# Sliding-window attention on one core: the value products of a unit directly ahead of the next unit's transposes

## The chip, the core and the metric

One core of one Trainium2 chip runs the whole program. The metric is the device time of one execution in microseconds (us); a kernel's time is the median of several runs. One execution was also recorded by the hardware profiler; times of single instructions come from there.

The engines are named as in the profile: PE (TensorE, matmuls; PEld is its weight load), DVE (VectorE), ACT (ScalarE), POOL (GpSimd) and SP (SyncE, which starts the loads). Each has an instruction queue of its own; between them semaphores keep the order of data.

## What is computed

The reference is a trunk of two layers on x of 1024 tokens by 1024 channels, in float32. The first is a gated MLP, cut here; the second is windowed attention with sinks:

```python
q, z = jnp.split(h @ w_in, 2, axis=-1)
...
logits = jnp.einsum('btkgd,bskd->bkgts', qb, kb).astype(jnp.float32) + alibi
valid = in_window & ((start - BLOCK + c) >= 0)
logits = jnp.where(valid, logits, -jnp.inf)
m = jnp.maximum(jnp.max(logits, axis=-1), sink)
p = jnp.exp(logits - m[..., None])
denom = jnp.sum(p, axis=-1) + jnp.exp(sink - m)
o = jnp.einsum('bkgts,bskd->btkgd', p.astype(vb.dtype), vb).astype(jnp.float32)
o = o / denom.transpose(0, 3, 1, 2)[..., None]
...
y = out * jax.nn.silu(z)
return y @ w_out
```

There are 16 query heads of 64 channels over 4 key/value heads, blocks of 128 queries, and a window of 128 keys, so a query sees its own block up to itself and the rest of its window in the block before.

## The kernel before

Large products are made with each operand split in a high and a low part, three matmuls in place of one (`mm3`, L169 to L171). The gated MLP takes the first three quarters of the time. In the attention stage, keys kh and kl, values vt and queries q are held in on-chip memory.

The attention of a half of the tokens (`attn`, L1114) is cut in eight units, one for each of two pairs of key/value heads (p) and four blocks of queries (b). Names carry b_p: s5_1 are the scores of block 5, pair 1. A unit has four steps.

- **Scores** (L1037 to L1075), in two halves gp of eight matmuls (L1058), over two banks of PSUM each (s5_1_00 and s5_1_01, then s5_1_10 and s5_1_11). DVE merges the window's two key blocks (copy_predicated, L1063) and takes bias and minimum (L1069), ACT the exponential (L1073).
- **Normalise** (L1078, L1079), on DVE.
- **Transposes** (L1081 to L1091): eight on PE (L1086) into two banks pt; ACT copies each bank into pc (L1087). POOL then masks pp, the earlier key block, out of pc (L1090), and pc itself (L1091). Units of blocks 0 have no pp.
- **Values** (L1093 to L1113): for each of two halves par of the array's columns a matmul with pc (L1105) and one with pp (L1107) into bank o; DVE multiplies by z (L1111), and the result is split for the output projection, q_hi on ACT (L105) and q_lo on DVE (L106).

The tiles s, o and pt draw their banks from one pool of four ("s"); the products that fill up have four others ("mm"). pc and pp share a tag with two buffers.

The steps of three units are interleaved. In turn i of the loop (L1125 to L1136) stand the first score half of unit i, the values of unit i-2, two calls of `more()`, the transposes of unit i-1, and the second score half and normalise of unit i. Each call of `more()` draws steps from a generator of other work: the projections of the next q and z, the shared keys and values, and at the end the output projection. These are the filling products: qz, pk and pv, ob, 128x512 or 128x256 matmuls. A unit's turn has mostly eighteen of them at each of the places where they are drawn.

The program written in this order goes through a scheduler, which may place instructions of an engine otherwise, by its own estimate of when operands are ready, and which sets the bank of each tile and the waits. What stands on each engine is shown below where it differs.

Of the kernel before, what the change touches and what calls it, by code (L numbers as in the profile page):

```python
# [34 lines left out]
def step(*gens):  # L35
    for g in gens:
        next(g, None)
# [13 lines left out]
def tile_yoco(  # L51
# [1062 lines left out]
    def attn(h, q, z, fill, total, late=0):  # L1114
        taken = [0, 0]
        n = 34 if late else 40

        def more():
            taken[0] += 1
            while taken[1] < min(total, total * taken[0] / n) + late * max(0, taken[0] - n):  # L1120
                taken[1] += 1
                step(fill)

        units = [Unit(b, p, q, z) for p in range(2) for b in range(4 * h, 4 * h + 4)]
        for i in range(len(units) + 2):  # L1125
            if i < len(units):
                units[i].scores(0)
            if 0 <= i - 2:
                units[i - 2].values()
            more()  # L1130
            more()
            if 0 <= i - 1 < len(units):
                units[i - 1].transposes()
            if i < len(units):
                units[i].scores(1)
                units[i].normalise()  # L1136
            more()
            more()
# [89 lines left out]
    q1 = pair("P3", "q1")  # L1228
    fill = chain(kv_phase(1, n1), q_phase(1, n1, q1), z_phase(1, n1, z1, 0, 4))
    attn(0, q0, z0, fill, 64)  # L1230
    drain(fill)

# [4 lines left out]

    fill = chain(z_phase(1, n1, z1, 4, 8), tail())
    attn(1, q1, z1, fill, 48, 2)
    drain(fill)  # L1240

# [60 lines left out]
```

## Time and profile before

| what | value |
| --- | --- |
| median of 3 runs | 1050.24 us (1049.72 to 1050.43) |
| the profiled execution, its own time | 1051.19 us |
| its span in the profile | 1049.4 us |
| granted clock of the core | 0.998 |
| first score matmul / last value block begins | 769.03 / 1002.36 us of the span |

The profiled execution is 0.95 us longer than the median of the runs, and 1.8 us of it lie around the span. An engine's busy time includes overlap between matmuls that follow each other, so how fast PE goes is read from the starts of two rows, and not from their lengths. In rows of the timeline the first number is the start in us from the span's beginning, the second the busy time in us; "x4" groups instructions of one kind.

### The profile page before, as it was taken

The numbers are of one execution on the slowest core, as the hardware profiler recorded it, in microseconds if no ns is written. First come the engines' busy times: TensorE is split into PE (matmuls) and PEld (weight loads), VectorE is DVE, ScalarE is ACT, GpSimd is POOL, SyncE is SP. The second block draws the span as 40 slices with busy tenths as digits, with TensorE's granted clock in tenths as the row PEclk, the third lists the DMA queues.
The fourth block names the chain that finished last, engine by engine and source line by source line (L and its number), as shares of the span: only waits on it lengthen the run. The fifth ranks groups of instructions, "written<-read, shape, count | busy, mean of one in ns | idle before, by whom it ended". The sixth has DMA issues, their size and how long they took to land.

```text
span 1049.4 us, 13678 instructions
## 1 busy us (share of the span) xinstructions
PE 1038.2 (99%) x4994; PEld 854.8 (81%) x4994; DVE 731.8 (70%) x1244; ACT 579.8 (55%) x998; POOL 199.5 (19%) x153
## 2 busy tenths in 40 slices
PE   9999999999999999999999999999999999999997
PEld 7878888888888888888888888888888777877776
DVE  6987566867768668677696587765247786667763
ACT  6584344565565465655444465654466665786631
POOL 0500003253442552530200000100001111011120
PEclk9999999999999999999999999999999999999999
DMA  8878242324333333247998543532322121211363
GB/s 309 271 262 292 101 171 94 116 101 146 126 117 120 123 134 116 101 140 265 320 354 282 195 167 93 200 102 82 99 81 66 56 81 61 81 61 62 121 220 121
DMA packets 80899, 157.56 MB, mean 150 GB/s; under 512 B 5824, under 2 KB 32704, under 8 KB 80832
## 3 DMA queue, kind: packets, MB, share of 16 engines
q1 hardware_dynamic: 76320, 148.01, 41.4%
q10 hardware_dynamic: 4512, 8.68, 2.3%
q8 instruction: 39, 0.64, 0.3%
q14 instruction: 28, 0.23, 0.1%
HBM read 125.21 MB, written 31.46 MB: 149 GB/s over the span
## 4 chain that ended last, share of the span: by engine, by line
PE 93%; DVE 3%; DMA 2%; ACT 1%; issue 0%; SPq 0%; DVEq 0%; POOLq 0%; ACTq 0%
PE qz L169 6%; PE ob L169 6%; PE ub L169 6%; PE qz L171 6%; PE ub L170 6%; PE ub L171 6%; PE ob L171 6%; PE ob L170 6%; PE qz L170 6%; PE s L1058 3%; PE uc L170 3%; PE uc L169 3%; PE uc L171 3%; PE sp L621 3%; PE oc L169 2%; PE oc L171 2%
## 5 line engine op out<-in xcount | busy, mean ns | idle before, releaser
L110 DVE SCALAR_TENSOR_TENSOR wlo<-raw_w,gn,whi 128x512 fp32r<-128x512 f32 x80 | 58.5, 757 | 62.2 <-ACT whi L109 62.0
L169 PE MATMUL qz<-n_hi,whi 128*128 128x512 f32 x256 | 100.9, 394 | 0.0
L171 PE MATMUL qz<-n_hi,wlo 128*128 128x512 f32 x256 | 99.8, 390 | 1.1 <-DVE wlo L110 1.1
L170 PE MATMUL qz<-n_lo,whi 128*128 128x512 f32 x256 | 99.9, 390 | 0.0
L109 ACT ACTIVATE whi<-raw_w,gn 128x512 fp32r<-128x512 f32 x80 | 54.8, 716 | 56.8 <-PE qz L170 36.6
L1073 ACT ACTIVATE pr<-pr,mx 128x129 f32<-128x129 f32 x128 | 50.1, 393 | 39.8 <-DVE mx L1069 39.8
L169 PEld LDWEIGHTS qz<-n_hi,whi 128*128 128x128 f32 x256 | 48.1, 188 | 15.8 <-issue 5.7
L105 ACT ACTIVATE uzhilo_g<-f 128x1024 fp32r<-128x1024 f32 x31 | 32.9, 1060 | 49.2 <-PE uc L171 43.3
L171 PEld LDWEIGHTS qz<-n_hi,wlo 128*128 128x128 f32 x256 | 48.0, 188 | 11.8 <-DVE wlo L110 1.5
L170 PEld LDWEIGHTS qz<-n_lo,whi 128*128 128x128 f32 x256 | 48.1, 188 | 9.3
L106 DVE TENSOR_TENSOR uzhilo_g<-f,uzhilo_g 128x1024 fp32r<-128x1024 f32 x31 | 38.6, 1245 | 19.9 <-ACT uzhilo_g L105 19.9
L209 ACT ACTIVATE uz_slots<-ub 128x512 f32<-128x512 f32 x48 | 28.3, 590 | 42.4 <-PE ub L171 39.2
L169 PE MATMUL ub<-T,whi_g 128*128 128x512 f32 x128 | 50.7, 396 | 0.0
L169 PE MATMUL ub<-T,uzhilo_g 128*128 128x512 f32 x128 | 50.5, 395 | 0.0
L171 PE MATMUL ub<-T,wlo_g 128*128 128x512 f32 x128 | 49.9, 390 | 0.0
L171 PE MATMUL ub<-T,uzhilo_g 128*128 128x512 f32 x128 | 49.9, 390 | 0.0
L170 PE MATMUL ub<-T,uzhilo_g 128*128 128x512 f32 x128 | 49.9, 390 | 0.0
L170 PE MATMUL ub<-T,whi_g 128*128 128x512 f32 x128 | 49.8, 389 | 0.0
L169 PE MATMUL uc<-T,uzhilo_g 128*128 128x512 f32 x124 | 48.9, 395 | 0.0
L170 PE MATMUL uc<-T,uzhilo_g 128*128 128x512 f32 x124 | 48.3, 389 | 0.0
L171 PE MATMUL uc<-T,uzhilo_g 128*128 128x512 f32 x124 | 48.3, 389 | 0.0
L105 ACT ACTIVATE whi_g<-raw_uz 128x1024 fp32r<-128x1024 f32 (+1 forms) x31 | 26.5, 854 | 36.8 <-PE ua L170 14.3
(334 smaller groups left out, 3078.3 us busy)
## 6 DMA issues: line engine op xcount, KB each, us to landing
raw_uz<-in_wuz_in_dram SPq DMA_DIRECT2D x32, 512.0 KB, 3.4
raw_w<-in_wqz_dram SPq DMA_DIRECT2D x32, 512.0 KB, 3.5
td<-uz_slots SPq DMA_DIRECT2D x56, 256.0 KB, 2.2
orawP2a<-td SPq DMA_DIRECT2D x28, 512.0 KB, 4.1
raw<-in_wv_in_dram SPq DMA_DIRECT2D x17, 512.0 KB, 4.8
vg<-vd SPq DMA_DIRECT2D x8, 1024.0 KB, 5.3
orawP2b<-in_wo_a_dram SPq DMA_DIRECT2D x16, 512.0 KB, 8.2
vraw<-in_wv_in_dram SPq DMA_DIRECT2D x13, 512.0 KB, 4.8
```

Source lines behind the costliest of these rows:

```text
L105: nc.scalar.activation(hi, src, AF.Copy)
L106: nc.vector.tensor_tensor(lo, src, hi.bitcast(F32), ALU.subtract)
L109: nc.scalar.activation(hi, src, AF.Copy, scale=g)
L110: nc.vector.scalar_tensor_tensor(lo, src, g, hi.bitcast(F32), ALU.mult, ALU.subtract)
L169: nc.tensor.matmul(out, lhsT=a_hi, rhs=b_hi, start=start, stop=False, skip_group_check=True)
L170: nc.tensor.matmul(out, lhsT=a_hi, rhs=b_lo, start=False, stop=False, skip_group_check=True)
L171: nc.tensor.matmul(out, lhsT=a_lo, rhs=b_hi, start=False, stop=stop, skip_group_check=True)
L209: nc.scalar.activation(out, a, AF.Copy)
L621: nc.tensor.matmul(psv[:, n], lhsT=d["vg"][:, 4 * j + n, i * P:(i + 1) * P], rhs=d["wc"], start=True, stop=True)
L1058: nc.tensor.matmul(pss[par][:, g, w0:256], lhsT=q[par][:, m, bs_], rhs=w[par][:, p, ks], start=g + k == 0, stop=g + k == 2, skip_group_che ...
L1073: nc.scalar.activation(pr[:, i], pr[:, i], AF.Exp, bias=mx[:, i:i + 1], scale=-1.0, accum_out=dn[:, i:i + 1])
```

## The change

The two calls of `more()` move ahead of the values of unit i-2. The first score half of unit i is now followed by filling products, then by the values of unit i-2 and directly by the transposes of unit i-1 and the second score half of unit i.

```diff
@@ -1125,10 +1125,10 @@
         for i in range(len(units) + 2):
             if i < len(units):
                 units[i].scores(0)
+            more()
+            more()
             if 0 <= i - 2:
                 units[i - 2].values()
-            more()
-            more()
             if 0 <= i - 1 < len(units):
                 units[i - 1].transposes()
             if i < len(units):
```

The first place is PE in the second pair of the first half: o1_1 are the values of unit 1_1, pt2_1 the transposes of 2_1, s3_1 the scores of 3_1, qz1 filling products (the number at the end of a name is a buffer's). Before, the values stand behind the first scores and ahead of the filling products:

```order
L1058 MATMUL s3_1_01_6766<-kh1_4959,q0_lo_4970 128x256
L1058 MATMUL s3_1_01_6766<-kl1_5556,q0_lo_4970 128x256
L1105 MATMUL o1_1_6785<-pc1_1_6693,vt_4968 64x512
L1107 MATMUL o1_1_6785<-pp1_1_6706,vt_4968 64x512
L1105 MATMUL o1_1_6785<-pc1_1_6693,vt_4968 64x512
L1107 MATMUL o1_1_6785<-pp1_1_6706,vt_4968 64x512
L169 MATMUL qz1_0_5_6540<-n1_hi_5306,whi31_6673 128x512
L170 MATMUL qz1_0_5_6540<-n1_lo_5307,whi31_6673 128x512
```

and, eighteen filling matmuls further, the transposes follow on these, with the second scores behind them:

```order
L170 MATMUL qz1_0_7_6542<-n1_lo_5307,whi31_6673 128x512
L171 MATMUL qz1_0_7_6542<-n1_hi_5306,wlo31_6674 128x512
L1086 MATMUL pt2_1_0_6824<-ident_82,pr2_1_6637 128x128 x4
L1086 MATMUL pt2_1_1_6830<-ident_82,pr2_1_6637 128x128 x4
L1058 MATMUL s3_1_10_6839<-kh0_4958,q0_hi_4969 128x256
L1058 MATMUL s3_1_10_6839<-kl0_4960,q0_hi_4969 128x256
L1058 MATMUL s3_1_11_6840<-kh1_4959,q0_lo_4970 128x256
L1058 MATMUL s3_1_11_6840<-kl1_5556,q0_lo_4970 128x256
L1058 MATMUL s3_1_10_6839<-kh0_4958,q0_hi_4969 128x256
L1058 MATMUL s3_1_10_6839<-kl0_4960,q0_hi_4969 128x256
```

In the changed kernel the same place reads:

```order
L170 MATMUL qz1_0_7_6534<-n1_lo_5307,whi31_6667 128x512
L171 MATMUL qz1_0_7_6534<-n1_hi_5306,wlo31_6668 128x512
L1105 MATMUL o1_1_6815<-pc1_1_6693,vt_4968 64x512
L1107 MATMUL o1_1_6815<-pp1_1_6706,vt_4968 64x512
L1105 MATMUL o1_1_6815<-pc1_1_6693,vt_4968 64x512
L1107 MATMUL o1_1_6815<-pp1_1_6706,vt_4968 64x512
L1086 MATMUL pt2_1_0_6824<-ident_82,pr2_1_6637 128x128 x4
L1086 MATMUL pt2_1_1_6830<-ident_82,pr2_1_6637 128x128 x4
L1058 MATMUL s3_1_10_6839<-kh0_4958,q0_hi_4969 128x256
L1058 MATMUL s3_1_10_6839<-kl0_4960,q0_hi_4969 128x256
L1058 MATMUL s3_1_10_6839<-kh0_4958,q0_hi_4969 128x256
L1058 MATMUL s3_1_10_6839<-kl0_4960,q0_hi_4969 128x256
```

The values stand between the last filling product and the transposes. The tiles of the second scores are also filled in another order: s3_1_10 wholly ahead of s3_1_11, where before they took turns.

The second place is PE further on, in the second half: o4_1 are the values of unit 4_1, ob0 filling products of the output projection. Before, twelve filling matmuls stand ahead of the first scores of 6_1, and the four value products stand together:

```order
L1058 MATMUL s6_1_01_7720<-kl1_5556,q1_lo_5850 128x256
L1058 MATMUL s6_1_00_7719<-kh0_4958,q1_hi_5849 128x256
L1058 MATMUL s6_1_00_7719<-kl0_4960,q1_hi_5849 128x256
L1058 MATMUL s6_1_01_7720<-kh1_4959,q1_lo_5850 128x256
L1058 MATMUL s6_1_01_7720<-kl1_5556,q1_lo_5850 128x256
L1105 MATMUL o4_1_7739<-pc4_1_7642,vt_4968 64x512
L1107 MATMUL o4_1_7739<-pp4_1_7655,vt_4968 64x512
L1105 MATMUL o4_1_7739<-pc4_1_7642,vt_4968 64x512
L1107 MATMUL o4_1_7739<-pp4_1_7655,vt_4968 64x512
L169 MATMUL ob0_1_0_7693<-whi44_7580,q0_hi_4969 128x512
L170 MATMUL ob0_1_0_7693<-wlo44_7581,q0_hi_4969 128x512
```

In the changed kernel the first scores of 6_1 follow at once on the second ones of 5_1, and of the values one product stands there alone:

```order
L1058 MATMUL s5_1_11_7659<-kl1_5556,q1_lo_5850 128x256
L1058 MATMUL s6_1_00_7719<-kh0_4958,q1_hi_5849 128x256
L1058 MATMUL s6_1_00_7719<-kl0_4960,q1_hi_5849 128x256
L1058 MATMUL s6_1_01_7720<-kh1_4959,q1_lo_5850 128x256
L1058 MATMUL s6_1_01_7720<-kl1_5556,q1_lo_5850 128x256
L1058 MATMUL s6_1_00_7719<-kh0_4958,q1_hi_5849 128x256
L1058 MATMUL s6_1_00_7719<-kl0_4960,q1_hi_5849 128x256
L1058 MATMUL s6_1_01_7720<-kh1_4959,q1_lo_5850 128x256
L1058 MATMUL s6_1_01_7720<-kl1_5556,q1_lo_5850 128x256
L1105 MATMUL o4_1_7761<-pc4_1_7642,vt_4968 64x512
L169 MATMUL ob0_1_0_7693<-whi44_7580,q0_hi_4969 128x512
L170 MATMUL ob0_1_0_7693<-wlo44_7581,q0_hi_4969 128x512
```

The other three come thirty filling matmuls later, ahead of the next unit's transposes:

```order
L170 MATMUL ob0_1_1_7694<-wlo45_7698,q0_hi_4969 128x512
L171 MATMUL ob0_1_1_7694<-whi45_7697,q0_lo_4970 128x512
L1107 MATMUL o4_1_7761<-pp4_1_7655,vt_4968 64x512
L1105 MATMUL o4_1_7761<-pc4_1_7642,vt_4968 64x512
L1107 MATMUL o4_1_7761<-pp4_1_7655,vt_4968 64x512
L1086 MATMUL pt5_1_0_7770<-ident_82,pr5_1_7592 128x128 x4
L1086 MATMUL pt5_1_1_7776<-ident_82,pr5_1_7592 128x128 x4
```

So the values of 4_1 are in two pieces in the changed kernel, and the filling matmuls that parted the two score blocks have moved behind the first piece.

The third place is DVE at the values of unit 2_0 (o2_0; wlo28 is a weight half of the filling products, L980 an evacuation of filling products). Before:

```order
L1069 ISA mx0_1_6378 128x1
L1111 TENSOR_TENSOR z0_0_5308<-o2_0_6401,z0_0_5308 128x4x128
L106 TENSOR_TENSOR q0_lo_4970<-z0_0_5308,q0_hi_4969 128x4x128
L110 SCALAR_TENSOR_TENSOR wlo28_6422<-raw_w28_6293,gn_80,whi28_6421 128x4x128 x2
L1046 COPY pr1_1_6507<-snk_4965 128x8
L980 SCALAR_TENSOR_TENSOR q1_hi_5849<-qz1_0_0_6219,qsc_4963,q1_hi_5849 64x512
L980 SCALAR_TENSOR_TENSOR q1_lo_5850<-qz1_0_0_6219,qsc_4963,q1_lo_5850 64x512
L1063 COPY_PREDICATED s0_1_10_6455<-mrg_4956,neg_4961 128x2x128
```

In the changed kernel:

```order
L1069 ISA mx0_1_6378 128x1
L110 SCALAR_TENSOR_TENSOR wlo28_6414<-raw_w28_6285,gn_80,whi28_6413 128x4x128 x2
L980 SCALAR_TENSOR_TENSOR q1_hi_5849<-qz1_0_0_6219,qsc_4963,q1_hi_5849 64x512
L980 SCALAR_TENSOR_TENSOR q1_lo_5850<-qz1_0_0_6219,qsc_4963,q1_lo_5850 64x512
L1111 TENSOR_TENSOR z0_0_5308<-o2_0_6431,z0_0_5308 128x4x128
L1046 COPY pr1_1_6507<-snk_4965 128x8
L106 TENSOR_TENSOR q0_lo_4970<-z0_0_5308,q0_hi_4969 128x4x128
L1063 COPY_PREDICATED s0_1_10_6455<-mrg_4956,neg_4961 128x2x128
L1063 COPY_PREDICATED s0_1_11_6456<-mrg_4956,neg_4961 128x2x128
```

The multiply L1111 has moved behind the weight split and the first evacuation, and stands nearer to the second scores of 0_1.

## Prediction, made before the changed kernel was run

> **What bounds the kernel now.** I read the page first: the busy shares, then the chain of work that ended last.
>
> ```profile
> PE 1038.2 (99%) x4994; PEld 854.8 (81%) x4994; DVE 731.8 (70%) x1244; ACT 579.8 (55%) x998; POOL 199.5 (19%) x153
> PE 93%; DVE 3%; DMA 2%; ACT 1%; issue 0%; SPq 0%; DVEq 0%; POOLq 0%; ACTq 0%
> ```
>
> TensorE is busy all the span and carries the chain. The next view is the table of stretches over the attention stage (span, PE, PEld, DVE, ACT, POOL, then the granted clock).
>
> ```profile
> core 0: us, PE busy (x) PEld busy (x) DVE busy (x) ACT busy (x) POOL busy (x), PEclk, DMA share, GB/s
> 800.00:820.00 20.00, 20.00 (x105) 15.77 (x105) 15.54 (x48) 13.10 (x39) 4.38 (x4) 1.00 0.17 54
> 900.00:920.00 20.00, 20.00 (x106) 15.97 (x105) 15.22 (x52) 12.68 (x44) 2.19 (x2) 1.00 0.24 79
> 980.00:1000.00 20.00, 20.00 (x100) 14.89 (x97) 14.26 (x34) 11.84 (x34) 4.69 (x5) 1.00 0.34 108
> ```
>
> PE fills 20.00 of 20.00 at clock 1.00 where the units run; no row of PE there names a wait. So nothing that the change could take out of a wait exists: the stage is the sum of its matmuls plus what is lost when PE passes from one kind of product to another. The change can gain only at such passages, and can lose wherever a product is now asked for before its operand or bank is ready. DVE is at about three quarters and ACT at two thirds, in order, so neither answers at once.
>
> The passages are read from start to start in the timeline of PE.
>
> ```profile
> 883.46 0.39 PE L170 MATMUL qz<-n_lo,whi 128*128 128x512 f32 x1
> 883.69 0.39 PE L171 MATMUL qz<-n_hi,wlo 128*128 128x512 f32 x1
> 884.01 1.08 PE L1105 MATMUL o<-pc,vt 128*64 128x512 f32 x4
> 884.92 1.03 PE L1107 MATMUL o<-pp,vt 128*64 128x512 f32 x4
> 885.88 0.50 PE L169 MATMUL qz<-n_hi,whi 128*128 128x512 f32 x1
> 886.22 0.40 PE L170 MATMUL qz<-n_lo,whi 128*128 128x512 f32 x1
> 886.46 0.40 PE L171 MATMUL qz<-n_hi,wlo 128*128 128x512 f32 x1
> ```
>
> A filling product starts 0.23 us after the one before. Into the value products it takes 0.32 (883.69 to 884.01), 0.09 too much; the block lasts 1.87 (to 885.88); and the first filling product behind it takes 0.34, 0.11 too much.
>
> **The change part by part.** The work is the same: as many instructions on each engine, in another order. SP's queue keeps its order.
>
> Regular passages. Before, a unit went scores, values, filling, transposes, scores; now scores, filling, values, transposes, scores. The entry of 0.09 stays (this row is itself one from filling into values). The 0.11 behind the values now falls on the first transpose. The difference is 0, with -0.11 x 15 = -1.6 as the good end (the load for the transposes hides) and, by the same size, +1.6 as the bad one. I take 0, since a transpose needs its 128x128 load just as the filling product did.
> The Trainium skill, "TensorEngine Tiling (Array Packing)", section "Key Properties", says that changing the tiling mode drains TensorE. By it the number of changes counts, and that number is the same before and after except at one unit (below), so the sum would be the same 0.
>
> The split unit. In the new order the values of unit 4_1 come apart: one product (pc, first column half), thirty filling matmuls, then the other three. The halves normally run side by side; a unit of block 0, which has only the pc pair, shows what one pass by itself lasts.
>
> ```profile
> 792.96 1.08 PE L1105 MATMUL o<-pc,vt 128*64 128x512 f32 x4
> 793.97 0.38 PE L169 MATMUL pv<-whi,n_hi 128*128 128x256 f32 x1
> ```
>
> The lone product costs 793.97 - 792.96 = 1.01, and the extra entry and exit 0.09 + 0.11: **+1.2 us**. Its remaining three still need two passes, so nothing comes back. Low end 0.2, if the three pair up better than I see.
>
> The same product comes too early. The twelve filling matmuls between scores(1) of 5_1 and scores(0) of 6_1 have gone behind it, so PE arrives soon after the transposes of 4_1, while POOL still masks. The rows of unit 5_1 give the offsets with ACT free: PE (first transposes, then the first, third, fifth of the eight score matmuls, then filling), ACT with the group of its line, POOL.
>
> ```profile
> 972.07 1.04 PE L1086 MATMUL pt<-ident,pr 128*128 128x128 f32 x8
> 972.86 0.36 PE L1058 MATMUL s<-kh,q_hi 128*128 128x256 f32 x1
> 973.18 0.28 PE L1058 MATMUL s<-kh,q_lo 128*128 128x256 f32 x1
> 973.41 0.28 PE L1058 MATMUL s<-kh,q_hi 128*128 128x256 f32 x1
> 973.89 0.40 PE L169 MATMUL ob<-whi,q_hi 128*128 128x512 f32 x1
> ```
> ```profile
> 972.78 1.09 ACT L1087 ACTIVATE pc<-pt 128x512 f32<-128x512 f32 x2 [0.61 <-PE pt L1086]
> L1087 ACT ACTIVATE pc<-pt x32: 573/595/601, 786.5 to 997.9; 128x512 f32<-128x512 f32 x32
> ```
> ```profile
> 973.94 1.10 POOL L1090 TENSOR_SCALAR_AFFINE_SELECT pp<-pc 128x1024 f32<-128x1024 f32 x1 [9.26 <-ACT pc L1087]
> 975.11 1.09 POOL L1091 TENSOR_SCALAR_AFFINE_SELECT pc<-pc 128x1024 f32<-128x1024 f32 x1
> ```
>
> POOL does pp first and ends pc at 976.20, 4.13 after the transposes began. PE reaches the lone product after 0.79 (transposes) + 1.03 + 1.03 (two score blocks) + 0.09 = 2.94. **+1.2 us** of stall; low end 0 if scores(0) of 6_1 are themselves late and take up the time, high end 2.2 if ACT's copies come a whole select later.
>
> The scores behind the transposes. The pool of banks for these tiles has four, and in the new built order five score blocks (units 0_1, 1_1, 3_1, 5_1, 6_1) take, for their second tile, the bank of the first transpose tile just before, instead of a bank long free. It is free when ACT's first copy ends: 972.78 + 0.595 = 973.38, 1.31 after the transposes began. The second tile is wanted by the third matmul (973.18, +1.11) in 0_1, 1_1 and 6_1 and by the fifth (973.41, +1.34) in 3_1 and 5_1. With 0.16 for the signal and the weight load behind the wait (an estimate, half of the 0.32 that the first two score matmuls take, 972.86 to 973.18), a third place costs 1.31 + 0.16 - 1.11 = 0.36 and a fifth 0.13, if ACT is free. It was not at three of them (the first transposes' row on PE, then ACT's rows, for the transposes ahead of 0_1, 1_1 and 3_1):
>
> ```profile
> 825.72 1.04 PE L1086 MATMUL pt<-ident,pr 128*128 128x128 f32 x8
> 826.62 0.68 ACT L976 ACTIVATE q_lo<-qz,qsc 64x512 fp32r<-64x512 f32 x1
> 827.33 1.09 ACT L1087 ACTIVATE pc<-pt 128x512 f32<-128x512 f32 x2
> 840.13 1.04 PE L1086 MATMUL pt<-ident,pr 128*128 128x128 f32 x8
> 840.60 0.62 ACT L105 ACTIVATE q_hi<-z 128x512 fp32r<-128x512 f32 x1
> 841.12 1.32 ACT L109 ACTIVATE whi<-raw_w,gn 128x512 fp32r<-128x512 f32 x2
> 842.46 1.09 ACT L1087 ACTIVATE pc<-pt 128x512 f32<-128x512 f32 x2
> 865.43 1.04 PE L1086 MATMUL pt<-ident,pr 128*128 128x128 f32 x8
> 867.88 0.69 ACT L976 ACTIVATE q_lo<-qz,qsc 64x512 fp32r<-64x512 f32 x1
> 868.59 1.09 ACT L1087 ACTIVATE pc<-pt 128x512 f32<-128x512 f32 x2
> ```
>
> At 825.72 the copy waited behind evacuations of the last filling products; these now finish 1.87 ahead of the transposes, so ACT is free: 0.36. At 840.13 the split q_hi goes behind the copy, but whi stays ahead: 842.46 - 0.52 = 841.94, plus 0.60 and 0.16, against 840.13 + 0.36 (the stall before it) + 1.11 = 841.60: 1.1. At 865.43 one of two evacuation pairs still stands ahead; the copy moves up from 868.59 by 0.5 and a pair of 1.4, to about 866.7 plus 0.76, against 866.77: about 0.7. Sum 0.36 + 1.1 + 0.7 + 0.13 + 0.36 = **+2.65 us**. The low end, ACT free everywhere, is 3 x 0.36 + 2 x 0.13 = 1.3; the high end, copies as late behind the transposes as before, has 827.33, 842.46 and 868.59, each plus 0.76, less 826.83, 841.24 and 866.77 at those places: 1.3 + 2.0 + 2.6, with 0.13 + 0.36 for the others 6.3.
>
> The multiply of the values. In most other units the second score tile takes the bank of the value product just finished, so it waits for DVE's multiply.
>
> ```profile
> 886.01 0.69 DVE L1111 TENSOR_TENSOR z<-o,z 128x512 f32<-128x512 f32 x1 [1.73 <-PE o L1107]
> 839.74 0.68 DVE L1111 TENSOR_TENSOR z<-o,z 128x512 f32<-128x512 f32 x1
> 832.67 1.09 PE L1105 MATMUL o<-pc,vt 128*64 128x512 f32 x4
> ```
>
> In these rows stand two multiplies of DVE and, for the second, the start of its value block on PE. With DVE free the multiply ends at 886.70, 2.69 after the block began at 884.01; the third score matmul comes at 1.87 + 1.11 = 2.98. It just fits; in the new order the multiply stands behind work that is done by then. I take **+0.2 us**, from 0 up to a single place like 839.74: 840.42 - 832.67 - 2.98 = 4.8.
>
> What follows on DVE and ACT (q_lo and q_hi of the values' output) comes a filling block later, and its reader is the output projection of a whole half later: nothing. At the end of the program the last filling products are as many.
>
> Sum: 1.2 + 1.2 + 2.65 + 0.2 = **+5.25 us**. The profiled execution took 1051.19 (span 1049.4), 0.95 above the median, so its own forecast is 1056.4; for the median 1050.24 + 5.25 = **1055.5**.
>
> **The rivals.** A measurement here tells about 0.2%, 2.1 us, from no change: below 1048.1 is faster, above 1052.3 slower.
>
> First, no difference: the waits are covered, since the score matmuls ahead of the copy start late enough or the copies come earlier, and only the split's 1.2 stays: 1051.4. For it: PE had no wait at all before, with scores behind the transposes there too. Against it: before, their banks had been released by values eighteen matmuls back. Chance 0.17.
>
> Second, faster: values and transposes are both 4-byte products on the same side of the filling, and the exit (0.11) and entry (0.09) vanish at fifteen units: -3.0. It decides only if the waits too are covered: 1047.2. For it: transposes behind filling showed no exposed load, so their load is hidden there. Against it: the o tiles are 128*64 and pt's 128*128. Chance 0.08.
> The Trainium skill, "TensorE: Matmul & The Clock Gate", section on the array's architecture, has the weight load pulled ahead of running matmuls; by that the 0.11 would vanish, -1.6. The 0.34 behind the values speaks against it here, since that load was not pulled ahead.
>
> Third, a bigger loss: DVE comes late to one multiply, as at 839.74, and PE stands 4.8, less the 0.2 already counted: 1060.1. It decides from the point at which DVE is more than 0.3 behind. Chance 0.13, and 0.62 for the forecast with its own range of 1052.5 to 1058.
>
> **How the numbers follow.** The likeliest case gives 1055.5. The range takes the no-change case's 1051.4 in and stops at 1050.8 (the split with the good end of the passages, 1050.24 + 1.2 - 1.6 = 1049.8, is half left out); upward it reaches 1059.2, where ACT's high end (6.3 instead of 2.65) ends: 1055.5 + 3.65 = 1059.2. Left out: the faster case and most of the late multiply. Faster 0.07, same 0.2 (the no-change case and some of the forecast's low end), slower 0.73.
>
> **What would show it.** In the new profile PE rows should name ACT's L1087 as what the scores waited for, at five units, some 0.1 to 1 us each, and POOL's L1091 ahead of the lone product of 4_1, about 1.2; the block of 4_1 should appear as 1.0 and 1.9. The start of the first transpose behind the values should be 1.87 after the block began, and the block itself 0.79 plus at most 0.11. The forecast is wrong if PE stays at 20.00 in every stretch with no wait (then the first rival, or the second if the whole stage is shorter), and short if waits on L1111 turn up.

## The result, and the profile after the change

The changed kernel takes 1057.49 us (median of 4 runs, 1057.26 to 1057.79) against 1050.34 (4 runs beside it): a ratio of 1.0066, 95% interval 1.0054 to 1.0078, so 7.15 us slower. The profiled execution took 1057.36 with a span of 1055.3, 5.9 above the 1049.4 of before; the rest of the 7.15 is that before's profiled run was slower than its median (0.85), that the changed kernel's was faster than its own (0.13), and 0.27 around the span. The last matmul starts at 1048.14 instead of 1042.26, and the first score matmul within 0.1 us of where it did, so the 5.9 us all arise in the attention stage.

In the page's first and fourth part PE still holds the span, but the chain of work that ended last has less of it.

```profile
PE 1041.5 (99%) x4994; PEld 854.1 (81%) x4994; DVE 735.7 (70%) x1244; ACT 579.7 (55%) x998; POOL 199.0 (19%) x153
PE 86%; DVE 6%; DMA 3%; ACT 2%; issue 1%; POOL 0%; SPq 0%; DVEq 0%; POOLq 0%; ACTq 0%
```

PE's share of the chain fell from 93% to 86%, and DVE's rose from 3% to 6%: there are now stretches in which the end is set by something PE waits for. The view of PE's waits, empty for this stage before, names three kinds (us in total, times, longest):

```profile
PE o L1105 <- POOL pc L1091: 1.5, 1, 1.5
PE qz L169 <- DVE q_lo L980: 0.8, 1, 0.8
PE s L1058 <- ACT pc L1087: 0.6, 2, 0.5
```

The view of the weight loads (PEld) shows the same waits and more, since a load can stand still without a matmul's row naming it:

```profile
PEld s L1058 <- ACT pc L1087: 1.8, 5, 0.7
PEld qz L169 <- DVE kl L1027: 0.8, 2, 0.5
```

Five score blocks wait for ACT's first copy, as predicted (their loads stand at 827.47, 843.55, 869.69, 964.64 and 979.11, in units 0_1, 1_1, 3_1, 5_1 and 6_1). The table of stretches shows where time is lost:

```profile
820.00:840.00 20.00, 19.06 (x93) 13.97 (x92) 17.02 (x44) 13.29 (x33) 2.62 (x2) 1.00 0.16 53
860.00:880.00 20.00, 19.53 (x98) 14.92 (x98) 17.78 (x41) 14.01 (x33) 2.18 (x2) 1.00 0.19 60
900.00:920.00 20.00, 20.00 (x109) 17.26 (x108) 13.14 (x44) 13.17 (x42) 2.18 (x2) 1.00 0.25 79
960.00:980.00 20.00, 18.41 (x93) 12.28 (x92) 13.85 (x37) 12.41 (x38) 2.90 (x3) 1.00 0.26 93
```

PE is 0.94 short of the full time in the first of these stretches, 0.47 in the second, 1.59 in the last, and full in others, as in the third. The busy time hides part of the loss, since a matmul's row is longer than its step: starts have to be compared. The timeline of PE at unit 4_1, and POOL's beside it:

```profile
966.06 0.28 PE L1058 MATMUL s<-kl,q_lo 128*128 128x256 f32 x1
967.79 1.07 PE L1105 MATMUL o<-pc,vt 128*64 128x512 f32 x2 [1.45 <-POOL pc L1091]
968.79 0.50 PE L169 MATMUL ob<-whi,q_hi 128*128 128x512 f32 x1
969.13 0.39 PE L170 MATMUL ob<-wlo,q_hi 128*128 128x512 f32 x1
```
```profile
965.15 1.09 POOL L1090 TENSOR_SCALAR_AFFINE_SELECT pp<-pc 128x1024 f32<-128x1024 f32 x1 [10.40 <-ACT pc L1087]
966.31 1.43 POOL L1091 TENSOR_SCALAR_AFFINE_SELECT pc<-pc 128x1024 f32<-128x1024 f32 x1
```

The lone product starts 1.73 after the last score matmul, where 0.21 is the usual step, and the moment is the end of POOL's mask (967.74): 1.5 us. Its block then lasts 1.00 by itself.

At the scores behind transposes, the longest wait is at unit 3_1, PE and ACT:

```profile
867.64 1.09 PE L1086 MATMUL pt<-ident,pr 128*128 128x128 f32 x8
868.94 0.28 PE L1058 MATMUL s<-kl,q_hi 128*128 128x256 f32 x1
869.69 0.39 PE L1058 MATMUL s<-kh,q_lo 128*128 128x256 f32 x1 [0.47 <-ACT pc L1087]
869.91 0.28 PE L1058 MATMUL s<-kl,q_lo 128*128 128x256 f32 x1
```
```profile
868.33 0.69 ACT L976 ACTIVATE q_lo<-qz,qsc 64x512 fp32r<-64x512 f32 x1
869.04 1.09 ACT L1087 ACTIVATE pc<-pt 128x512 f32<-128x512 f32 x2
```

The first copy ends near 869.6 and the fifth score matmul starts at 869.69, 0.63 later than a step of 0.12 would put it; the next step is 0.10 too long as well.

The third wait was not in the prediction. Filling products stand still in the turn of unit 1_1, PE and DVE:

```profile
834.45 0.39 PE L171 MATMUL qz<-n_hi,wlo 128*128 128x512 f32 x1
835.62 0.47 PE L169 MATMUL qz<-n_hi,whi 128*128 128x512 f32 x1 [0.78 <-DVE q_lo L980]
```
```profile
832.72 1.23 DVE L1079 TENSOR_TENSOR pr<-pr,dn 128x1024 f32<-128x1024 f32 x1
833.96 0.74 DVE L980 SCALAR_TENSOR_TENSOR q_hi<-qz,qsc,q_hi 64x512 fp32r<-64x512 f32 x1
834.72 0.76 DVE L980 SCALAR_TENSOR_TENSOR q_lo<-qz,qsc,q_lo 64x512 fp32r<-64x512 f32 x1
```

The filling matmul needs a bank of the projection before it, which DVE empties by the pair ending at 835.48, behind the normalise of 0_1. The next two banks are late as well, by about 0.2 each, so the 24 filling matmuls there take 6.96 instead of 5.57. Before, the values of 3_0 lay between the scores of 1_1 and these products, and PE arrived 1.87 later.

A place without waits shows the regular passage, filling to values to transposes to scores:

```profile
923.06 0.39 PE L171 MATMUL qz<-n_hi,wlo 128*128 128x512 f32 x1
923.38 1.09 PE L1105 MATMUL o<-pc,vt 128*64 128x512 f32 x4
925.25 1.09 PE L1086 MATMUL pt<-ident,pr 128*128 128x128 f32 x8
926.10 0.36 PE L1058 MATMUL s<-kh,q_hi 128*128 128x256 f32 x1
```

The entry takes 0.32 and the value block 1.87, as before; the transposes take 0.85 (925.25 to 926.10) where they took 0.79 behind filling products.

### The profile page after: what moved, and what is told of

It reads as the page before. It is cut to its first block, busy times and chain, and to the rows that moved or that the text cites. A ratio compares the mean times of both kernels' runs of the same rounds, so it can differ in the third digit from the quotient of the medians.

```text
span 1055.3 us, 13677 instructions
## 1 busy us (share of the span) xinstructions
PE 1041.5 (99%) x4994; PEld 854.1 (81%) x4994; DVE 735.7 (70%) x1244; ACT 579.7 (55%) x998; POOL 199.0 (19%) x153
## 4 chain that ended last, share of the span: by engine, by line
PE 86%; DVE 6%; DMA 3%; ACT 2%; issue 1%; POOL 0%; SPq 0%; DVEq 0%; POOLq 0%; ACTq 0%
PE ob L169 6%; PE ub L169 6%; PE ub L171 6%; PE ub L170 6%; PE ob L171 6%; PE ob L170 6%; PE qz L169 5%; PE qz L171 5%; PE qz L170 5%; PE uc L169 3%; PE uc L170 3%; PE uc L171 3%; PE sp L621 3%; PE s L1058 2%; PE oc L171 2%; PE oc L169 2%
## 5 line engine op out<-in xcount | busy, mean ns | idle before, releaser
L110 DVE SCALAR_TENSOR_TENSOR wlo<-raw_w,gn,whi 128x512 fp32r<-128x512 f32 x80 | 58.9, 763 | 63.6 <-ACT whi L109 63.4
L109 ACT ACTIVATE whi<-raw_w,gn 128x512 fp32r<-128x512 f32 x80 | 54.8, 716 | 60.1 <-PE qz L170 34.3
L1090 POOL TENSOR_SCALAR_AFFINE_SELECT pp<-pc 128x1024 f32<-128x1024 f32 x14 | 15.7, 1123 | 164.6 <-ACT pc L1087 164.6
```

Of the source, the lines that this page charges most:

```text
L109: nc.scalar.activation(hi, src, AF.Copy, scale=g)
L110: nc.vector.scalar_tensor_tensor(lo, src, g, hi.bitcast(F32), ALU.mult, ALU.subtract)
L1090: nc.gpsimd.affine_select(pp, pc, [[0, 8], [-1, P]], ALU.is_ge, 0.0, base=-1, channel_multiplier=1)
```

## The experiments

My theory was that the loss sits at single places, where an operand or a bank comes too late. The rival that had to be told apart from it is an even price: every passage from values to transposes costs the same. Beside the medians I use the profile: the distance from the first score matmul to the last matmul of the program, "the stage", 273.23 us before and 279.17 in the changed kernel, so 5.94 longer. A stage comes from one execution. The medians, each less the kernel before that was measured beside it, give differences between kernels that lie up to 1.6 us from those of the stages, so the price of a single place is read from the rows and the stage, and the medians bear on sums of several microseconds.

**The two halves of the tokens.** The new order in one of them.

```diff
+            moved = h == 0        # half1: h == 1
+            if 0 <= i - 2 and not moved:
+                units[i - 2].values()
             more()
             more()
-            if 0 <= i - 2:
+            if 0 <= i - 2 and moved:
                 units[i - 2].values()
```

> The new order in the first half of the tokens alone, the old one in the second. Theory of single places (the loss sits at a few turns where an operand or a bank is late): here the scores' waits for ACT's copies in units 0_1, 1_1 and 3_1 (0.3, 0.4, 0.7 us), the filling products' wait for DVE's evacuations at 835.6 (1.2), a short one at 803 (0.3), together about +2.8 us against before, as the start of s4_0_0 has it (894.1 before, 897.0 after): 1053.1. Rival, an even price (every passage from values to transposes costs the same, 7.1 us over fifteen turns or 0.48 each): the first half has eight of them, the second eight, so about half in each, 1053.8. The two differ in what PE waits for: in the rival no row names ACT's copy or DVE's evacuation.

> The new order in the second half of the tokens alone. Theory of single places: the split values of 4_1 (1.2 us), their wait for POOL (1.5), two waits of scores for ACT's copies (0.3 and 0.4), less a little at the regular passages: about +3.1 us, 1053.4. Rival, an even price of 0.48 for each of eight turns: +3.8, 1054.1, with nothing special at 4_1.

Measured: 1054.22 us with the first half (before beside it 1050.89; ratio 1.0032, 1.002 to 1.0044) and 1054.51 with the second (1.0033, 1.0022 to 1.0045). The stages are 276.27 and 276.21, so 3.04 and 2.98 longer: together 6.02 for the 5.94 of the whole. The sizes alone (3.0 each) don't tell the two apart. The waits do: of the first half

```profile
PE qz L169 <- DVE q_lo L980: 0.8, 1, 0.8
PE s L1058 <- ACT pc L1087: 0.7, 2, 0.5
```

and of the second

```profile
PE o L1105 <- POOL pc L1091: 1.4, 1, 1.4
```

Each half keeps its own waits from the whole change, so they belong to places.

**Single turns taken back.** Three kernels keep the old place in one turn each, with the edit of the halves and another test, for the values of 7_0, of 3_0 and of 1_1:

```diff
+            moved = not (h == 1 and i == 5)    # keep70
+            moved = not (h == 0 and i == 5)    # keep30
+            moved = not (h == 0 and i == 7)    # keep11
```

> The change everywhere but in the one turn that holds the values of 7_0 (second half, sixth turn): they keep their old place. In the built order the values of 4_1 then stand together again, behind 21 filling matmuls. Theory of single places: the split (1.2 us) and the wait for POOL (1.5) go, and with them the wait of s5_1 for ACT's copy (0.3): 3.0 less, 1054.5. Rival, an even price: one turn of fifteen, 0.5 less, 1057.0. Second rival, the wait for POOL only moves to the next product that needs ACT or DVE: 1.2 less, 1056.3.

> The change everywhere but in the one turn that holds the values of 3_0 (first half, sixth turn): they stand ahead of their filling products again, and so between the scores of 1_1 and the products that wait for DVE's evacuations of the last projection (L980). Theory: the values' 1.87 us cover that evacuation, so the wait of 0.8 to 1.2 us goes, and the wait of s1_1 for ACT's copy (0.4) too: about 1.5 less, 1056.0. Rival, DVE is late there anyway and the wait is only moved: 1057.4. Rival, an even price: 0.5 less, 1057.0.

> The change everywhere but in the turn that holds the values of 1_1 (first half, eighth turn). Theory: the wait of the scores of 3_1 for ACT's first copy goes (0.63 in the row, 0.1 behind it) and nothing else: 0.7 less than the changed kernel, in the profile's span 1054.6 against 1055.3. Rival: ACT is late for reasons of its own and the wait is found at the same place or at the next filling products: no change.

Measured: keeping 7_0 in place 1053.96 (ratio to before 1.0028, 1.0018 to 1.0039), stage 275.91, so 3.26 less than the changed kernel: the theory's 3.0 and not the even price's 0.5. The waits at 4_1 are gone, and the only ones named in PE's rows are those of the first half:

```profile
PE qz L169 <- DVE q_lo L980: 0.7, 1, 0.7
PE s L1058 <- ACT pc L1087: 0.6, 2, 0.5
```

Keeping 3_0 in place: 1055.8 (1.0045, 1.0028 to 1.0061), stage 277.52, 1.65 less. Here are PE and DVE where the wait was:

```profile
833.96 1.09 PE L1105 MATMUL o<-pc,vt 128*64 128x512 f32 x4
835.83 0.50 PE L169 MATMUL qz<-n_hi,whi 128*128 128x512 f32 x1
```
```profile
835.32 0.76 DVE L980 SCALAR_TENSOR_TENSOR q_lo<-qz,qsc,q_lo 64x512 fp32r<-64x512 f32 x1
836.10 0.74 DVE L980 SCALAR_TENSOR_TENSOR q_hi<-qz,qsc,q_hi 64x512 fp32r<-64x512 f32 x1
```

DVE is no faster here; its pair ends at 836.08. What changed is what PE does meanwhile, 1.87 us of values. In the changed kernel six filling matmuls found their bank free and the seventh stopped; here the seventh comes after 836.08.

Keeping 1_1 in place: the wait for ACT's copy at 3_1 is gone from the rows, but the stage is 278.88, only 0.29 less than the changed kernel, where 0.7 was expected. The median is 1056.61 (1.0049, 1.0031 to 1.0067). The 42 filling matmuls behind these scores take 10.00 instead of 9.62, and the weight load of one of them says why:

```profile
875.57 0.39 PE L169 MATMUL qz<-n_hi,whi 128*128 128x512 f32 x1
875.99 0.19 PEld L171 LDWEIGHTS qz<-n_hi,wlo 128*128 128x128 f32 x1 [0.45 <-DVE wlo L110]
875.99 0.50 PE L171 MATMUL qz<-n_hi,wlo 128*128 128x512 f32 x1
```

PE arrives earlier and waits for the low weight half that DVE makes (L110): 0.19 in this step and 0.11 in the next. So the place is right, and half of its price went to another wait, which lay under the first one.

**All places with a wait taken back** (`keep5`). Five turns keep the old place. Of the sixteen turns with values, eleven then have the new place, and in nine of these transposes follow on the values (the last turn of each half has none), so the "ten" of the expectation is nine:

```diff
+            moved = i not in ((2, 4, 5, 7) if h == 0 else (5,))
```

> The change, but five turns keep the old place of the values: those of 0_0, 2_0, 3_0 and 1_1 in the first half, 7_0 in the second, that is, the turns at which the new kernel's rows show a wait. Theory of single places: all waits go; what is left are ten turns in which values stand ahead of transposes at no cost (the first transpose 0.06 later, the filling 0.11 earlier): the time of before within 0.2%, or up to 0.5 us less, 1050.4 to 1051.4 against 1050.9. Rival, an even price of 0.48 a turn: ten turns, +4.8, 1055.7.

Measured: 1050.63 us against 1050.67 for before (11 and 15 runs; ratio 1.0, 0.9991 to 1.0009), the stage 273.18 against 273.23. The view of PE's waits is empty, and the table of stretches is full again, but for 0.03 in the stretch from 860:

```profile
960.00:980.00 20.00, 20.00 (x112) 16.16 (x111) 17.66 (x48) 14.55 (x39) 4.48 (x4) 1.00 0.33 101
```

The even price (1055.7, and more with eleven turns) is out. But "all waits go" was not right: the weight loads show a wait at the place where `keep11` has it,

```profile
873.29 0.19 PEld L171 LDWEIGHTS qz<-n_hi,wlo 128*128 128x128 f32 x1 [0.45 <-DVE wlo L110]
```

and the 42 filling matmuls around it take 10.01, 0.39 more than in the changed kernel. The equal time is a balance: up to the first scores of the second half `keep5` is 0.29 behind the kernel before, and over the second half, where six of the nine turns stand, it gains 0.34, some 0.05 a turn.

**Was POOL the price at 4_1?** (`mask2`) POOL's mask of pc is made twice for this unit, which happens to make the scheduler put the values of 4_1 together, behind the thirty filling matmuls; nothing else moves on PE.

```diff
-            nc.gpsimd.affine_select(pc, pc, [[0, 8], [1, P]], ALU.is_ge, 0.0, base=0, channel_multiplier=-1)
+            for _ in range(2 if self.id == "4_1" else 1):
+                nc.gpsimd.affine_select(pc, pc, [[0, 8], [1, P]], ALU.is_ge, 0.0, base=0, channel_multiplier=-1)
```

> The changed kernel with POOL's mask of pc (L1091) made twice for unit 4_1 alone: 1.1 us more work, the same values. In the built order the values of 4_1 then stand together behind the 30 filling matmuls, and no other product of PE moves. If the split and POOL are the whole price of that place, 1.2 + 1.5 = 2.7 less than the changed kernel: 1054.8. Rival: the filling products now follow the scores of 6_1 at once, and wait for DVE's evacuation of the projection's tiles (yb, L1164), as they did for 1.4 to 1.6 us with the values behind the transposes; POOL's wait was a cover for that: only the split goes, 1.2 less, 1056.3.

Measured: 1055.22 (ratio to before 1.004, 1.0025 to 1.0055), stage 277.82, 1.35 less than the changed kernel, with 1.1 us more of POOL's work. The times don't decide: by the medians, each against its own before, the kernel is 2.9 less than the changed one, nearer to the theory's 2.7 than to the rival's 1.2. The rows do, for the rival. Those of PE, of DVE and of POOL are

```profile
965.85 0.28 PE L1058 MATMUL s<-kl,q_lo 128*128 128x256 f32 x1
967.56 0.50 PE L169 MATMUL ob<-whi,q_hi 128*128 128x512 f32 x1 [1.43 <-DVE yb L1165]
```
```profile
966.83 0.68 DVE L1165 TENSOR_TENSOR yb<-ob,gpb 128x512 f32<-128x512 f32 x1
```
```profile
966.10 2.59 POOL L1092 TENSOR_SCALAR_AFFINE_SELECT pc<-pc 128x1024 f32<-128x1024 f32 x2
```

(the added line moves the numbers behind it by one). PE stands still for the same 1.7 us, now for the bank that DVE's evacuation yb empties, and starts at 967.56 while POOL works until 968.69. In the changed kernel this evacuation ends at much the same time:

```profile
967.04 0.68 DVE L1164 TENSOR_TENSOR yb<-ob,gpb 128x512 f32<-128x512 f32 x1
```

There POOL's wait and the lone product behind it (to 968.79) covered it. Taking POOL's wait away with the lone product left in its place was not run: by these rows the filling could then start near 967.8 instead of 968.79, an estimate of 1.0 gained and 0.5 still lost. The 3.26 of the place is thus the split (1.2) and one wait of about 1.5 that has two causes, both from twelve filling matmuls that no longer part the scores of 5_1 from those of 6_1; the rest is the wait of s5_1 (0.3) and that of s6_1 (0.36), which went with them (their sum is 0.1 more than 3.26).

**Two other places for the values.** `behind` has them after the transposes, ahead of the second scores; `between` has one call of `more()` on each side. Against the changed kernel:

```diff
             more()
             more()
-            if 0 <= i - 2:
-                units[i - 2].values()
             if 0 <= i - 1 < len(units):
                 units[i - 1].transposes()
+            if 0 <= i - 2:
+                units[i - 2].values()
```

and

```diff
             more()
-            more()
             if 0 <= i - 2:
                 units[i - 2].values()
+            more()
```

> Values behind the transposes instead of ahead of them, ahead of the second scores; filling still ahead of both. Theory: the values' 1.87 us cover ACT's copies (wanted 0.2 to 0.7 us later in the changed kernel), and the values of 4_1 stand together, so these waits and the one for POOL go; DVE's evacuations at the projection's end keep their wait (about 1.2, since nothing lies between scores and filling there). Filling matmuls that the built order puts between two score tiles cost some 0.1 each at nine places. 1050.9 + 1.2 + 0.9 = 1053.0. Rival, that the banks of the scores then wait for DVE's multiply of the values, which ends 2.7 after the block began: 0.5 or more at each of twelve units, 1057 and above.

> One call of more() ahead of the values and one behind, so that filling stands on both sides. Theory: transposes, copies and multiply have filling around them as before, so no wait of scores for ACT or POOL; each turn has one passage more (into and out of the values from filling: 0.2 instead of 0.2 less the 0.09 between scores and values), and the built order has the values of 1_0 split by 24 filling matmuls (1.2). 1050.9 + 1.2 + up to 0.5 = 1052.4. Rival, an even price for values behind filling: 0.48 a turn, 1058.

Both expectations missed. `behind` takes 1056.56 (1.0058, 1.0045 to 1.0072), its stage 279.45, 6.2 over before and not 2.1. The waits for ACT's copies stayed, since ACT was late again; PE and ACT at unit 3_1:

```profile
869.73 0.40 PE L171 MATMUL qz<-n_hi,wlo 128*128 128x512 f32 x1
870.60 0.39 PE L1058 MATMUL s<-kh,q_lo 128*128 128x256 f32 x1 [0.47 <-ACT pc L1087]
```
```profile
868.50 0.68 ACT L976 ACTIVATE q_lo<-qz,qsc 64x512 fp32r<-64x512 f32 x1
869.96 1.09 ACT L1087 ACTIVATE pc<-pt 128x512 f32<-128x512 f32 x2
```

With the transposes directly behind the filling, the evacuations of the filling (L976) stand ahead of the copy, as they did before the change: the 1.87 that the values give behind the transposes they had given ahead of them. It also has the wait for yb at 968.65, and two of filling products for DVE's evacuations of the keys (L1027) and of q (L980). The multiply, my rival there, is named in no wait of PE. `between` takes 1054.67 (1.0037, 1.0024 to 1.0051), its stage 276.85, 3.6 over before and not 1.5: no wait of scores, but the one for DVE's evacuation is there (835.06, 1.28 after the matmul ahead of it), and the lone product of 1_0 waits for POOL:

```profile
801.24 1.07 PE L1105 MATMUL o<-pc,vt 128*64 128x512 f32 x2 [0.36 <-POOL pc L1091]
835.06 0.47 PE L169 MATMUL qz<-n_hi,whi 128*128 128x512 f32 x1 [0.90 <-DVE q_lo L980]
```

I had not looked whether DVE's evacuation would find cover there: twelve filling matmuls stand now between the first scores of 1_1 and the values, and the seventh comes as early as in the changed kernel.

**The copies made twice** (one run).

```diff
                 nc.scalar.activation(pc[:, 4 * gp:4 * gp + 4], pt, AF.Copy)
+                nc.scalar.activation(pc[:, 4 * gp:4 * gp + 4], pt, AF.Copy)
```

> The changed kernel with each of ACT's copies of the transposes (L1087) made twice, the second over the first. Theory: where the scores wait for the first copy, the wait grows by the copy's pace of 0.5 us: 0.32 to 0.8 at unit 0_1 and 0.36 to 0.9 at 1_1. In the built order the values of 4_1 are not split, so that 1.2 goes, and POOL's wait there with it, as 30 filling matmuls lie ahead. Rival, that the wait is for something else that ends with the copy (the transposes' own end): no change at these two.

Measured: 1056.15, stage 277.66. It does not answer its question. At 0_1 PE waits 1.17 us too long, but for the multiply of the values (828.96 to 829.65), not for the copy; at 1_1 nothing waits. The waits say that the scores now have other banks. What it does show is the third rival of the prediction at work at a price of about 1.2:

```profile
829.71 0.33 PE L1058 MATMUL s<-kh,q_lo 128*128 128x128 f32 x1 [1.00 <-DVE z L1112]
```

## Why the prediction was right, and where its sum was off

The forecast was slower by 5.25, the result is 7.15 by the medians and 5.9 in the profile's span, within the range; the mechanism is the one given, single late places and a split block, which `keep5` and the single turns show. That the sum comes so close is in part luck: 1.7 us of waits that it lacks are offset by terms that came out 1.15 lower on balance. Term by term:

| term | predicted | measured in the rows |
| --- | --- | --- |
| split of 4_1 | 1.2 | 1.2 (1.00, 0.11 behind it, 0.09 into the second piece) |
| wait at the lone product | 1.2 | 1.5 |
| scores waiting for ACT's copies, five units | 2.65 | 2.1 |
| multiply of the values | 0.2 | 0 |
| regular passages | 0 | about -0.7 |
| filling waiting for DVE's evacuations | none | about 1.4, and 0.3 at 803 |

Together the last column makes 5.8, for the 5.94 by which the stage is longer. The split is exact. Of POOL's wait the mechanism was right and the size 0.3 short: the masks end 4.70 after the transposes began, predicted 4.13 (ACT's copies came 0.25 later, and the second mask took 1.43 instead of 1.09), and the scores ahead of the lone product were 0.3 later too. But the low end, 0 if the scores of 6_1 are themselves late, missed what would be behind it: `mask2` shows a wait of filling products for DVE's yb under it. So POOL is what PE waited for, but without POOL the place would not have come free.

Of the five copies, 0_1 came out as worked (0.32 against 0.36), and 3_1 too (0.73 against 0.7). 1_1 did not: 1.1 was predicted and 0.36 came. By the rows the waits for DVE ahead of it had moved these transposes to 842.12, and ACT, done with whi (L109) at 842.53, was free by the time it was needed; no run separates the two. 5_1 was 0.3 instead of 0.13, with two of ACT's sums of squares (L183) ahead of the copy, which began 0.25 late. `keep11` shows that removing such a wait does not give back all of it.

The regular passages sit inside the stated bounds: the transposes behind values pay 0.06, and the eighteen filling matmuls, which no longer follow on values, take 4.11 instead of 4.22 (without the entry of 0.09 that both orders have), so 0.05 less a turn. Fourteen turns have this passage, not the fifteen of the prediction: -0.7. `keep5` shows it over its second half.

The step that failed is the one on what filling products need: I costed nothing for their own banks. The values had stood between the scores and the next filling products, and so, at the end of a projection, had covered the evacuations of its banks; the move took that cover away. I had looked for who waits behind the moved block, and not for who had been hidden by it in the old place. `keep30` shows it: with the values back, DVE ends no earlier and PE does not wait.

Both rivals at or below no change fell by the same rows. (The faster one's 1047.2 left out the split, which its own text does not remove; with it the time would be 1048.4, no longer below the 1048.1 that it needed. And the low bound, with half of the passages' 1.6 left out, would be 1050.6 and not 1050.8; nothing hangs on it.) A rival of late multiplies did not come in this kernel, though it did in the one with two copies.

On the Trainium skill's "TensorEngine Tiling (Array Packing)", "Key Properties": the count of changes of mode is the same except at 4_1, and the nine turns of `keep5` gain only some 0.05 each, which fits the rule without singling it out. The Trainium skill's statement in "TensorE: Matmul & The Clock Gate", in the section on the array's architecture, that weight loads are pulled ahead, gave -0.11 a turn; the measured 0.05 lies between that and 0. In the rows the load of the transposes is not pulled ahead behind values (it starts at 925.25, with its matmul), while behind filling products, in the kernel before, it started at 922.25 for a matmul at 922.47.

## What to carry to other kernels

On an engine that never waits, a block that is moved has two effects: its followers come closer to what they wait for, and what it had covered in its old place lies open. Look through both, for every reader of a bank or operand that another engine still has in hand, those of unrelated filling work too. And under a wait there may be a second one, as at 4_1 and at 3_1: take the first away before its size is promised as a gain, and look at the weight loads too, where a wait can stand that no matmul's row names.

## What the runs showed of the hardware that was not expected

Transposes directly behind value products begin as late as filling products do (1.87 after the block of values began), but pay 0.06 us over the block of eight, not the 0.11 of a filling product. In both the first load starts only with its matmul, so what makes the difference is not shown. POOL's mask of 128x1024, mostly 1.09 us, took 1.43 at 966.31 in the changed kernel and 1.96 at the longest before; no run here tells why.
